# Delta keys kept unnormalised, with one transposition instead of two, and gate tiles copied out of their bank by ScalarE

## The chip, the cores and the metric

The kernel runs on one core of a Trainium2 chip. The metric is the device time of one execution in microseconds, taken as the median of several runs. A core has TensorE (PE, with its weight loads as PEld), VectorE (DVE), ScalarE (ACT), GpSimd (POOL) and SyncE (SP), which issues the DMAs. Each works through its own queue of instructions in order.

## The reference

One hybrid decoder layer for 512 tokens of width 2048, in float32. A modulated RMS norm gives h; one wide product of h feeds a sliding-window attention branch, a gated delta-rule branch and two merge gates; the branches are projected, merged and added to x. What matters here is the delta-rule branch, with 16 key heads and 32 value heads of 128:

```python
d_qkv = causal_conv_silu(d_qkv, conv_w)
dq, dk, dv = jnp.split(d_qkv, [DN_KEY, 2 * DN_KEY], axis=-1)
dq = jnp.repeat(l2_norm(dq...), rep, axis=2)
dk = jnp.repeat(l2_norm(dk...), rep, axis=2)     # x * rsqrt(sum(x * x) + EPS), by token and head
beta = jax.nn.sigmoid(db)
...
L = jnp.where(strict, einsum(k_beta, k) * decay, 0.0)     # in chunks of 64 tokens
t_inv = triangular_solve(eye + L, eye)
u = t_inv @ v_beta
w = t_inv @ (k_beta * jnp.exp(g)[..., None])
...
v_new = u_c - w_c @ S                                      # scan over the chunks
o = qd_c @ S + qk_c @ v_new
S = S * gl_c + kd_c.T @ v_new
...
o = rms_norm(o, dn_norm_w) * jax.nn.silu(dz)
```

Every key is divided by its own norm over the 128 channels, which depends on the token alone.

## The kernel before, in words

The work goes in stages: a start-up (norm, modulation, the first four key tiles), the keys stage (`delta_keys`), the attention stage, the heads stage (`delta_heads`) and a tail with the large output products. In the first stages the unit is a channel tile: 128 output channels by all 512 tokens, 16 steps of the contraction with three products each (L280 to L282: high by high, high by low, low by high part), so 48 matmuls of 128x512 into one PSUM bank. Two banks take turns, so the third tile may start only when the first one's bank has been read. A weight tile of 1 MB is loaded by SP (L213, two or three buffers), and split in halves by ScalarE (whi, L68) and VectorE (wlo, L69), three halves deep.

After every second contraction step `pump` runs (L98): it lets the background work take one step. Everything beside the products is a generator that says with `yield n` after how many pumps its next step is due; the solve, the sums of weight quadrants (q, L1505 to L1516) and the modulation gate (gate_bc, L1863) run at a pace of their own. Each engine's queue is then ordered when the kernel is built; in the keys stage TensorE's instructions may be reordered against the program too.

The keys stage takes 12 key tiles (four more come from start-up) and 18 output-gate tiles (z). First come four gates, then the keys 4 to 7 back to back, then keys and gates in turn, then the gates that are left.

A key tile (`keys`, L752) goes through these steps. The convolution (`conv`, L655): ScalarE scales by one tap (L659), VectorE adds three shifted taps out of the bank (L662), then tanh (L667) and a product (L669) give y, channels by tokens. Four transpositions give ptk, tokens by channels, in PSUM; ScalarE sums its squares (L801). VectorE takes the inverse root in eleven small operations (L763 to L81, rk). ScalarE writes k, the tokens scaled by rk (L768, four activations). Four more transpositions give ptkT, and ScalarE copies it to kT (L776), the normalised key, channels by tokens. The product pkk of kT with itself (L783) is multiplied by VectorE into the decay tiles E of two heads (L786), and the results go to scratch memory (L793, L794). k and kT go there too, for the heads stage. The decay tiles are loaded by SP as broadcasts of g_rows (L806), masked by GpSimd (L811), and run through exponentials by ScalarE (L817). ptk, ptkT and pkk share a PSUM pool of two buffers.

A gate tile (`z_gate`, L316): ScalarE takes the tanh of half the bank (L320), VectorE multiplies (tanh + 1) by the bank (L322), and the result is stored (L324). The same function serves the gates of the later stages, with another pool tag.

The solve (L819) inverts the triangular matrices of 16 heads at a time on VectorE: it loads beta by rows (bet, L831) and the tiles lt_d, multiplies the columns by minus beta (nb), and at the end the inverse by beta. The heads stage loads k, kT and the inverses, turns each value tile into token order (vt, L900, one copy by ScalarE), and scans four blocks of 128 tokens.

Of the kernel before, what the change touches and what calls it, by code (L numbers as in the profile page):

```python
# [7 lines left out]
F32 = mybir.dt.float32  # L8
F32R = mybir.dt.float32r
I32 = mybir.dt.int32  # L10
AF = mybir.ActivationFunctionType
ALU = mybir.AluOpType
# [4 lines left out]
P = 128  # L17
T = 512
D = 2048
KT = D // P  # L20
NTB = T // P
EPS = 1e-6
KH = 16
VH = 32
QH = 32
HD = 64
# [26 lines left out]
class Layer:  # L53
# [262 lines left out]
    def z_gate(self, h, ps):  # L316
        nc = self.nc
        pool, tag, bufs = self.zpool
        th = pool.tile([P, T], F32, tag=tag, name="zth", bufs=bufs)
        nc.scalar.activation(th, ps, AF.Tanh, scale=0.5)  # L320
        yield 1
        nc.vector.scalar_tensor_tensor(out=th, in0=th, scalar=1.0, in1=ps, op0=ALU.add, op1=ALU.mult)  # L322
        yield 3
        self.behind(nc.sync.dma_start(out=self.z_d[h], in_=th))  # L324

# [253 lines left out]
    def gates(self, sp):  # L579

        nc, a, dnc = self.nc, self.a, self.dnc
# [14 lines left out]
            nc.tensor.transpose(pb[:, c, :], ba[:, c * P : (c + 1) * P], self.ident)  # L596
        nc.vector.tensor_copy(out=bd, in_=pb[:, :, 0 : 2 * VH])
        nc.vector.tensor_tensor(out=bd, in0=pb[:, :, 2 * VH :], in1=bd, op=ALU.add)
        beta = self.beta = dnc.tile(S, F32, name="beta")
        e = sp.tile(S, F32, name="ge")  # L600
        nc.scalar.activation(e, bd[:, :, 0:VH], AF.Exp, scale=-1.0)
        nc.vector.tensor_scalar(out=e, in0=e, scalar1=1.0, scalar2=None, op0=ALU.add)
# [69 lines left out]
    def delta_keys(self):  # L672
        tc = self.tc
        dram = self.dram
        self.lt_d = dram.tile([2, 2, 16, 4, HD, HD], F32, name="lt_d")
        self.lab_d = dram.tile([VH, HD, 4, HD], F32, name="lab_d")
        self.ta_d = dram.tile([2, 16, 4, HD, HD], F32, name="ta_d")
        self.ts_d = dram.tile([2, 2, 16, 4, HD, HD], F32, name="ts_d")
        self.kT_d = dram.tile([KH, P, T], F32, name="kT_d")
        self.k_d = dram.tile([KH, P, T], F32, name="k_d")  # L680
        self.o_d = dram.tile([VH, P, T], F32, name="o_d")
        with ExitStack() as sa:
            self.ptp = sa.enter_context(tc.tile_pool(name="ptp", bufs=2, space=PSUM, reuse_waits="tile"))
            self.zpool = (sa.enter_context(tc.tile_pool(name="gwk", bufs=1, reuse_waits="tile")), "zth", 1)
            wk = sa.enter_context(tc.tile_pool(name="dnA", bufs=2, reuse_waits="tile"))
            gp = sa.enter_context(tc.tile_pool(name="gates", bufs=1, reuse_waits="tile"))
            gates = self.gates(gp)
            self.go(gates, next(gates))
            gt = sa.enter_context(tc.tile_pool(name="gatew", bufs=1, reuse_waits="tile"))
            self.beside(self.gate(gt), 0.26, "gate")  # L690
            kr = sa.enter_context(tc.tile_pool(name="kraw", bufs=1, reuse_waits="tile"))
            self.third_raw(kr, self.last_key)
            self.due += [self.split_half] * 2
            self.keys_done = []
            for g in range(NST):
                self.go(self.keys(wk, g, self.acc_k[g]), 10 + 8 * g)
            for h in ZAHEAD[:NFIRST]:
                self.z_tile(h)
            self.solved = []
            self.solves = self.paced(self.solve_all(), 0.41)  # L700
            ws = sa.enter_context(tc.tile_pool(name="wsumk", bufs=1, reuse_waits="tile"))
            sums = self.paced(self.weight_sums(ws, [0], 12.5), 1.0)
            rwk = sa.enter_context(tc.tile_pool(name="rwk", bufs=1, reuse_waits="tile"))
            self.go(self.rope_tables(rwk, rwk), 40)
            for kind, j in self.mixed():
                if kind == "k":
                    self.go(self.keys(wk, j, self.channel_tile(f"k{j}")), 0)
                else:
                    self.z_tile(j)
            self.drain("gate")  # L710
            self.drain_slow(sums)
            self.drain_live()
# [39 lines left out]
    def keys(self, wk, g, ps):  # L752

        nc = self.nc
        y = wk.tile([P, T], F32, tag="y", name="y", bufs=3)
        yield from self.conv(wk, ps, 16 + g, y)
        yield 2
        pt = self.ptp.tile([P, T], F32, tag="tp", name="ptk")
        self.transpose4(pt, lambda c: y[:, c * P : (c + 1) * P])
        ss = self.sumsq(wk, pt)  # L760
        yield 3
        E = [self.decay_load(wk, 2 * g + e) for e in range(2)]
        nc.vector.tensor_scalar(out=ss, in0=ss, scalar1=EPS, scalar2=None, op0=ALU.add)  # L763
        rk = self.rsqrt(wk, ss, NTB, "rk")
        yield 4
        k = wk.tile([P, NTB, P], F32, tag="k", name="k")
        for c in range(NTB):
            nc.scalar.activation(k[:, c, :], pt[:, c * P : (c + 1) * P], AF.Copy, scale=rk[:, c : c + 1])  # L768
        for e in range(2):
            self.decay_mask(E[e])  # L770
        yield 4
        pt = self.ptp.tile([P, T], F32, tag="tp", name="ptkT")
        self.transpose4(pt, lambda c: k[:, c, :])
        nc.sync.dma_start(out=self.k_d[g], in_=k.rearrange("p c d -> p (c d)"))
        kT = wk.tile([P, T], F32, tag="kT", name="kT")
        nc.scalar.copy(out=kT, in_=pt)  # L776
        for e in range(2):
            self.decay_exp(E[e], 2 * g + e)
        yield 2
        pk = self.ptp.tile([P, NTB, P], F32, tag="tp", name="pkk")  # L780
        for c in range(NTB):
            sl = slice(c * P, (c + 1) * P)
            self.pe(nc.tensor.matmul(pk[:, c, :], lhsT=kT[:, sl], rhs=kT[:, sl], start=True, stop=True))  # L783
        nc.sync.dma_start(out=self.kT_d[g], in_=kT)
        for e in range(2):
            nc.vector.tensor_tensor(out=E[e], in0=pk, in1=E[e], op=ALU.mult)  # L786
        yield 2
# [31 lines left out]
    def solve(self, wk, b, eng):  # L819
# [3 lines left out]
            yield 1.0  # L823
        A = wk.tile([P, HD, HD], F32, tag="A", name="A", bufs=1)
        bet = wk.tile([P, HD], F32, tag="bet", name="bet", bufs=1)
        for k2 in range(2):
            s = slice(k2 * HD, (k2 + 1) * HD)
            nc.sync.dma_start(
                out=A[s].rearrange("u j i -> u (j i)"), in_=self.lt_d[b, k2].rearrange("h c j i -> (h c) (j i)")
            )  # L830
            nc.sync.dma_start(  # L831
                out=bet[s],
                in_=self.b_rows.rearrange("h (c k i) -> k (h c) i", c=4, k=2)[k2, b * HD : (b + 1) * HD, :],
            )
        yield 8.0
        nb = wk.tile([P, HD], F32, tag="nbet", name="nbet", bufs=1)
        self.behind(eng.tensor_scalar(out=nb, in0=bet, scalar1=-1.0, scalar2=None, op0=ALU.mult))
        for j in range(0, HD, 16):
            s = slice(j, j + 16)
# [52 lines left out]
    def values(self, wk, g, e, ps, st):  # L892
        nc = self.nc
        y = wk.tile([P, T], F32, tag="y", name="yv", bufs=3)
        yield from self.conv(wk, ps, 32 + 2 * g + e, y)
        yield 3
        pt = self.ptp.tile([P, T], F32, tag="tp", name="ptv")
        self.transpose4(pt, lambda c: y[:, c * P : (c + 1) * P])
        vt = wk.tile([P, NTB, P], F32, tag="vt", name="vt", bufs=4)
        nc.scalar.copy(out=vt.rearrange("p c d -> p (c d)"), in_=pt)  # L900
        st[f"v{e}"] = vt

    def queries(self, wk, g, ps, st):
# [1056 lines left out]
```

## Time and profile before

| | us |
|---|---|
| median of three runs (lowest, highest) | 2884.59 (2880.28, 2886.27) |
| the profiled execution | 2872.44 |
| its span from first to last instruction | 2870.7 |

The profiled execution has a granted TensorE clock of 0.988 in the mean. The page gives the busy time of each engine with its share of the span; the tables by stretch give the busy time of each engine within a window, the number of instructions in brackets, then the granted TensorE clock, the share in which the 16 DMA engines are busy, and GB/s. A line of the waits reads: the engine and line that waited, what released it, the sum in us, the number of waits, the longest. A line of the timeline is start and duration in us, engine, line, operation, output and inputs, and in square brackets the idle time before it. A line of a group gives the count, the busy sum, the mean in ns of one, and the idle time before them. Matmuls overlap each other, so the distance of their starts is what one costs, not the duration.

### The profile page before, as it was taken

The numbers are of one execution on the slowest core, as the hardware profiler recorded it, in microseconds if no ns is written. First come the engines' busy times: TensorE is split into PE (matmuls) and PEld (weight loads), VectorE is DVE, ScalarE is ACT, GpSimd is POOL, SyncE is SP. The second block draws the span as 40 slices with busy tenths as digits, with TensorE's granted clock in tenths as the row PEclk, the third lists the DMA queues.
The fourth block names the chain that finished last, engine by engine and source line by source line (L and its number), as shares of the span: only waits on it lengthen the run. The fifth ranks groups of instructions, "written<-read, shape, count | busy, mean of one in ns | idle before, by whom it ended". The sixth has DMA issues, their size and how long they took to land.

```text
span 2870.7 us, 39644 instructions
## 1 busy us (share of the span) xinstructions
PE 2769.7 (96%) x13864; PEld 2237.7 (78%) x13864; DVE 2212.2 (77%) x3594; ACT 1318.3 (46%) x2649; POOL 139.6 (5%) x124
## 2 busy tenths in 40 slices
PE   8999898999999999999989999998999999999999
PEld 6788676777777777778878888777878878788887
DVE  7887787788778778899777777758666878887876
ACT  5565342234544434434534444445444645454543
POOL 0010000011000001101000001000000000000000
PEclk9999999999999999999999999999999999999999
DMA  9889888554565458999999999966798999998875
GB/s 401 346 272 286 294 301 275 163 188 136 182 174 186 160 169 294 289 317 305 313 300 309 301 309 293 297 193 205 251 312 311 325 324 327 352 347 279 293 250 189
DMA packets 332652, 776.39 MB, mean 270 GB/s; under 512 B 88066, under 2 KB 112258, under 8 KB 287394
## 3 DMA queue, kind: packets, MB, share of 16 engines
q1 hardware_dynamic: 332452, 773.86, 79.9%
q8 instruction: 109, 1.79, 0.2%
q14 instruction: 91, 0.75, 0.1%
HBM read 588.84 MB, written 182.66 MB: 269 GB/s over the span
## 4 chain that ended last, share of the span: by engine, by line
PE 44%; DMA 7%; DVE 3%; issue 1%; SPq 1%; ACT 1%; POOL 0%; DVEq 0%; POOLq 0%; ACTq 0%
PE m L281 9%; PE m L282 9%; PE m L280 9%; PE mm L280 4%; PE mm L282 4%; PE mm L281 4%; DMA s_d<-q 3%; DMA q<-in_w_q 1%; DVE wlo L69 1%; PE pv L1004 1%; PE pp L994 1%; PE pod L1021 1%; DMA b_d<-o 0%; PE pod L1017 0%; PE pod L1020 0%
## 5 line engine op out<-in xcount | busy, mean ns | idle before, releaser
L69 DVE TENSOR_TENSOR wlo<-raw,whi 128x1024 fp32r<-128x1024 f32 x588 | 721.2, 1228 | 347.6 <-ACT whi L68 334.8
L68 ACT CAST whi<-raw 128x1024 fp32r<-128x1024 f32 x588 | 617.0, 1051 | 758.3 <-PE m L282 352.4
L280 PE MATMUL mm<-hh,whi 128*128 128x512 f32 x2016 | 832.0, 413 | 12.9 <-DVE zth L322 12.9
L282 PE MATMUL mm<-hh,wlo 128*128 128x512 f32 x2016 | 795.1, 394 | 0.0
L281 PE MATMUL mm<-hl,whi 128*128 128x512 f32 x2016 | 792.9, 393 | 0.0
L280 PEld LDWEIGHTS mm<-hh,whi 128*128 128x128 f32 x2016 | 383.2, 190 | 102.0 <-DVE zth L322 15.6
L282 PEld LDWEIGHTS mm<-hh,wlo 128*128 128x128 f32 x2016 | 382.3, 190 | 84.5 <-issue 0.2
L281 PEld LDWEIGHTS mm<-hl,whi 128*128 128x128 f32 x2016 | 383.8, 190 | 70.8 <-issue 0.5
L1511 DVE TENSOR_TENSOR q<-q,q 128x512 f32<-128x512 f32 x384 | 270.5, 704 | 48.0 <-DMA q<-in_w_q 34.5
L849 DVE TENSOR_TENSOR atmp<-A 128x62 f32<-128x62 f32 (+30 forms) x124 | 109.6, 884 | 0.5
L857 DVE TENSOR_TENSOR A<-A,atmp 128x62 f32<-128x62 f32 (+30 forms) x124 | 107.8, 869 | 0.5
L811 POOL TENSOR_SCALAR_AFFINE_SELECT E<-E 128x512 f32<-128x512 f32 x64 | 55.9, 884 | 1020.1 <-DMA E<-g_rows 927.6
L817 ACT ACTIVATE E<-E,neg_g 128x128 f32<-128x128 f32 x256 | 82.2, 400 | 16.3 <-POOL E L811 13.2
L280 PE MATMUL m<-whi,hh 128*128 128x512 f32 x192 | 77.3, 404 | 8.1 <-ACT whi L68 6.7
L281 PE MATMUL m<-wlo,hh 128*128 128x512 f32 x192 | 76.6, 399 | 1.3 <-DVE wlo L69 1.3
L1022 ACT COPY osb<-pod 128x256 f32<-128x256 f32 x64 | 23.7, 371 | 117.2 <-PE pod L1021 93.1
L1009 ACT ACTIVATE vs<-pv,kd 128x128 f32<-128x128 f32 x96 | 30.1, 365 | 102.5 <-PE pv L1004 102.1
L282 PE MATMUL m<-whi,hl 128*128 128x512 f32 x192 | 75.9, 396 | 0.0
L662 DVE SCALAR_TENSOR_TENSOR yv<-mm,convh,yv 128x511 f32<-128x511 f32 (+2 forms) x96 | 71.3, 743 | 1.0
L281 PE MATMUL m<-wlo,f2h 128*128 128x512 f32 x160 | 62.5, 391 | 0.9 <-DVE wlo L69 0.9
L1807 ACT ACTIVATE sm<-sm,mx,rs 128x128 f32<-128x128 f32 x128 | 61.5, 482 | 2.9 <-DVE mx L1802 2.4
L280 PE MATMUL m<-whi,f1h 128*128 128x512 f32 x160 | 62.7, 392 | 0.0
(436 smaller groups left out, 4781.8 us busy)
## 6 DMA issues: line engine op xcount, KB each, us to landing
raw<-in_w_ch SPq DMA_DIRECT2D x126, 1024.0 KB
q<-in_w_q SPq DMA_DIRECT2D x384, 256.0 KB
s_d<-q SPq DMA_DIRECT2D x384, 256.0 KB
raw<-s_d SPq DMA_DIRECT2D x96, 1024.0 KB
raw<-in_w_q SPq DMA_DIRECT2D x72, 1024.0 KB
wa<-in_w_ada_ss SPq DMA_DIRECT2D x32, 1024.0 KB
gw<-in_w_ada_gate SPq DMA_DIRECT2D x16, 1024.0 KB
E<-g_rows SPq DMA_DIRECT2D x64, 256.0 KB
```

Of the source, the lines that this page charges most:

```text
L68: h = self.nc.scalar.copy(out=hi, in_=src)
L69: l = self.nc.vector.tensor_tensor(out=lo, in0=src, in1=hi.bitcast(F32), op=ALU.subtract)
L280: self.pe(nc.tensor.matmul(ps, lhsT=wh, rhs=xh, start=first, stop=False))
L281: self.pe(nc.tensor.matmul(ps, lhsT=wh, rhs=xl, start=False, stop=False))
L282: self.last_mm = self.pe(nc.tensor.matmul(ps, lhsT=wl, rhs=xh, start=False, stop=last))
L662: nc.vector.scalar_tensor_tensor(out=y[:, s:], in0=ps[:, : T - s], scalar=w[:, j : j + 1], in1=y[:, s:], op0=ALU.mult, op1=ALU.add)
L811: self.last_mask = self.nc.gpsimd.affine_select(out=E, in_=E, pattern=[[0, NTB], [1, P]], compare_op=ALU.is_ge, fill=NEG, base=0, channel_ ...
L817: self.nc.scalar.activation(E[:, c, :], E[:, c, :], AF.Exp, bias=self.neg_g[:, c, h : h + 1])
L849: eng.tensor_tensor(out=t, in0=A[:, m : m + 1, m + 1 :].to_broadcast([P, m, n]), in1=A[:, :m, m : m + 1].to_broadcast([P, m, n]), op=ALU.mult,
L857: self.behind(eng.tensor_tensor(out=A[:, :m, m + 1 :], in0=A[:, :m, m + 1 :], in1=t, op=ALU.add))
L1511: self.behind(self.nc.vector.tensor_tensor(out=q[f], in0=q[x], in1=q[y], op=ALU.add))
L1807: nc.scalar.activation(t, t, AF.Exp, scale=r[:, h : h + 1], bias=mx[:, h : h + 1], accum_out=den[:, h : h + 1])
```

## The change

The key is no longer divided by its norm n. Scratch memory and the heads stage get the raw key, and what this changes is put right in other places: beta is divided by n squared (sum of squares plus EPS) wherever it is used in the inverse, and the values are multiplied by n. The scan's new values then come out divided by n, which the raw key makes good where it meets them (in the state's update and in the product with the queries).

In `keys`: the raw y goes to kT_d right after its transposition; ScalarE writes one plain copy k of ptk right after the sums of squares; VectorE computes n (knorm), 1/n squared (inv) and scales the two heads' columns of neg_beta in place; SP stores inv twice, once per head, as 512 single words each; the second transposition and kT go; pkk is the product of y with itself; and the yields become 2, 3, 2, 2, 2, 2 where they were 2, 3, 4, 4, 2, 2. y gets a fourth buffer. In the solve two more loads bring inv, and one more product makes bet. In the heads stage vt is written by four scaled activations, one per block of 128 tokens. In `z_gate`, in the keys stage alone, ScalarE copies the bank to zc right after the tanh, and VectorE's product reads zc.

```diff
@@ z_gate
         nc.scalar.activation(th, ps, AF.Tanh, scale=0.5)
+        if tag == "zth":
+            z = pool.tile([P, T], F32, tag="zc", name="zc", bufs=bufs)
+            nc.scalar.copy(out=z, in_=ps)
+        else:
+            z = ps
         yield 1
-        nc.vector.scalar_tensor_tensor(out=th, in0=th, scalar=1.0, in1=ps, op0=ALU.add, op1=ALU.mult)
+        nc.vector.scalar_tensor_tensor(out=th, in0=th, scalar=1.0, in1=z, op0=ALU.add, op1=ALU.mult)
@@ keys
-        y = wk.tile([P, T], F32, tag="y", name="y", bufs=3)
+        y = wk.tile([P, T], F32, tag="y", name="y", bufs=4)
...
         self.transpose4(pt, lambda c: y[:, c * P : (c + 1) * P])
+        nc.sync.dma_start(out=self.kT_d[g], in_=y)
         ss = self.sumsq(wk, pt)
+        k = wk.tile([P, NTB, P], F32, tag="k", name="k")
+        nc.scalar.copy(out=k.rearrange("p c d -> p (c d)"), in_=pt)
         yield 3
...
         rk = self.rsqrt(wk, ss, NTB, "rk")
-        yield 4
-        k = wk.tile([P, NTB, P], F32, tag="k", name="k")
-        for c in range(NTB):
-            nc.scalar.activation(k[:, c, :], pt[:, c * P : (c + 1) * P], AF.Copy, scale=rk[:, c : c + 1])
+        nc.vector.tensor_tensor(out=self.knorm[:, :, g], in0=ss, in1=rk, op=ALU.mult)
+        inv = wk.tile([P, NTB], F32, tag="inv", name="inv")
+        nc.vector.reciprocal(out=inv, in_=ss)
+        both = inv.unsqueeze(2).to_broadcast([P, NTB, 2])
+        nb = self.neg_beta[:, :, 2 * g : 2 * g + 2]
+        nc.vector.tensor_tensor(out=nb, in0=nb, in1=both, op=ALU.mult)
+        nc.sync.dma_start(out=self.k_d[g], in_=k.rearrange("p c d -> p (c d)"))
+        for e in range(2):
+            nc.sync.dma_start(out=self.inv_d[2 * g + e].rearrange("(c p) -> p c", p=P), in_=inv)
+        yield 2
         for e in range(2):
             self.decay_mask(E[e])
-        yield 4
-        pt = self.ptp.tile([P, T], F32, tag="tp", name="ptkT")
-        self.transpose4(pt, lambda c: k[:, c, :])
-        nc.sync.dma_start(out=self.k_d[g], in_=k.rearrange("p c d -> p (c d)"))
-        kT = wk.tile([P, T], F32, tag="kT", name="kT")
-        nc.scalar.copy(out=kT, in_=pt)
+        yield 2
         for e in range(2):
             self.decay_exp(E[e], 2 * g + e)
...
-            self.pe(nc.tensor.matmul(pk[:, c, :], lhsT=kT[:, sl], rhs=kT[:, sl], start=True, stop=True))
-        nc.sync.dma_start(out=self.kT_d[g], in_=kT)
+            self.pe(nc.tensor.matmul(pk[:, c, :], lhsT=y[:, sl], rhs=y[:, sl], start=True, stop=True))
@@ solve
+            for dst, rows in ((bet, self.b_rows), (nb, self.inv_d)):
...
+        self.behind(eng.tensor_tensor(out=bet, in0=bet, in1=nb, op=ALU.mult))
         self.behind(eng.tensor_scalar(out=nb, in0=bet, scalar1=-1.0, scalar2=None, op0=ALU.mult))
@@ values
-        nc.scalar.copy(out=vt.rearrange("p c d -> p (c d)"), in_=pt)
+        for c in range(NTB):
+            nc.scalar.activation(vt[:, c, :], pt[:, c * P : (c + 1) * P], AF.Copy, scale=self.knorm[:, c, g : g + 1])
```

More of the change, by code (lines that the diff above doesn't have):

```diff
@@ L598, in gates @@
         nc.vector.tensor_tensor(out=bd, in0=pb[:, :, 2 * VH :], in1=bd, op=ALU.add)
-        beta = self.beta = dnc.tile(S, F32, name="beta")
+        beta = sp.tile(S, F32, name="beta")
         e = sp.tile(S, F32, name="ge")
@@ L680, in delta_keys @@
         self.k_d = dram.tile([KH, P, T], F32, name="k_d")
+        self.inv_d = dram.tile([VH, T], F32, name="inv_d")
+        self.knorm = self.dnc.tile([P, NTB, KH], F32, name="knorm")
         self.o_d = dram.tile([VH, P, T], F32, name="o_d")
@@ L825, in solve @@
         bet = wk.tile([P, HD], F32, tag="bet", name="bet", bufs=1)
+        nb = wk.tile([P, HD], F32, tag="nbet", name="nbet", bufs=1)
         for k2 in range(2):
@@ L830, in solve @@
             )
[L831 to L834, printed above, removed]
+            for dst, rows in ((bet, self.b_rows), (nb, self.inv_d)):
+                nc.sync.dma_start(
+                    out=dst[s], in_=rows.rearrange("h (c k i) -> k (h c) i", c=4, k=2)[k2, b * HD : (b + 1) * HD, :]
+                )
         yield 8.0
-        nb = wk.tile([P, HD], F32, tag="nbet", name="nbet", bufs=1)
+        self.behind(eng.tensor_tensor(out=bet, in0=bet, in1=nb, op=ALU.mult))
         self.behind(eng.tensor_scalar(out=nb, in0=bet, scalar1=-1.0, scalar2=None, op0=ALU.mult))
```

## The prediction

> **What bounds the kernel now.** I read the page first, then the busy time by stretches, then TensorE's waits in the stretch that the change touches.
>
> ```profile
> span 2870.7 us, 39644 instructions
> PE 2769.7 (96%) x13864; PEld 2237.7 (78%) x13864; DVE 2212.2 (77%) x3594; ACT 1318.3 (46%) x2649; POOL 139.6 (5%) x124
> ```
>
> TensorE is busy for 96% of the span, so a gain can only be work taken off TensorE or idle time given back to it. The stretches are the keys stage while keys come back to back (120 to 280 us), the keys stage with keys and output gates in turn (280 to 540, with 400 to 440 out of its middle), and the heads stage (1085 to 1960).
>
> ```profile
> core 0: us, PE busy (x) PEld busy (x) DVE busy (x) ACT busy (x) POOL busy (x), PEclk, DMA share, GB/s
> 120.00:280.00 160.00, 158.02 (x776) 130.23 (x775) 126.76 (x261) 96.05 (x255) 14.49 (x18) 1.00 0.87 284
> 280.00:540.00 260.00, 230.97 (x1017) 186.99 (x1016) 198.44 (x288) 90.21 (x209) 14.54 (x16) 0.95 0.83 273
> 400.00:440.00 40.00, 36.01 (x171) 29.61 (x170) 37.47 (x53) 16.15 (x37) 1.25 (x2) 1.00 0.91 304
> 1085.00:1960.00 875.00, 846.88 (x4611) 698.95 (x4609) 667.25 (x1172) 385.68 (x1024) 79.19 (x64) 0.99 0.89 290
> ```
>
> In the first stretch TensorE is full (158 of 160 us): there the bound is its own work. In the second it is idle for 29 of 260 us and its clock is granted at 0.95 in the mean. VectorE fills 76% of that stretch, the DMA engines 83%, ScalarE 35%. The waits of TensorE from 120 to 540 us say where the idle time goes (in all, number of waits, longest).
>
> ```profile
> PE mm L280 <- DVE zth L322: 12.9, 4, 5.8
> PE ptk L329 <- DVE E L786: 8.7, 1, 8.7
> PE pkk L783 <- ACT kT L776: 4.7, 5, 1.7
> PE ptkT L329 <- ACT k L768: 2.1, 2, 1.8
> PE pkk L783 <- DVE E L786: 1.6, 1, 1.6
> ```
>
> These 30 us are the whole idle time of the stage. Each of the five has a place in the diff: the accumulation bank of a gate tile is freed by VectorE (L322); the second transposition waits for ScalarE's scaled copy k, and the product pkk for the copy kT; and three users (ptk, ptkT, pkk) share two PSUM buffers, so that ptk waits for VectorE to read an older pkk (L786).
>
> **The change part by part.** *The second transposition.* One set of four costs TensorE this:
>
> ```profile
> 204.05 0.40 PE L282 MATMUL mm<-hh,wlo 128*128 128x512 f32 x1
> 204.29 0.60 PE L329 MATMUL ptkT<-ident,k 128*128 128x128 f32 x4
> 204.64 0.48 PE L280 MATMUL mm<-hh,whi 128*128 128x512 f32 x1
> 204.96 0.40 PE L281 MATMUL mm<-hl,whi 128*128 128x512 f32 x1
> 205.19 0.40 PE L282 MATMUL mm<-hh,wlo 128*128 128x512 f32 x1
> ```
>
> From 204.05 to 204.96 is 0.91 us, in which two products start; the next two starts lie 0.23 apart where nothing comes between (205.19 after 204.96), so the set costs 0.91 - 0.46 = 0.45 us. Sixteen keys: **-7.2 us**, all of it on the path where TensorE is full.
>
> *The waits behind it.* pkk reads y, ready since before the first transposition, and waits for neither k nor kT: 4.7 + 2.1 = **-6.8 us**. ptk and pkk are the only users of the two PSUM buffers but for the gate sums, so a ptk no longer needs an older pkk to be read: 8.7 + 1.6 = **-10.3 us**.
>
> *The gate tile's copy.* ScalarE copies the tile out right behind the tanh, and the bank is free then, not after VectorE's product. The longest of the four waits:
>
> ```profile
> 474.62 0.58 ACT L320 ACTIVATE zth<-mm 128x512 f32<-128x512 f32 x1
> ```
>
> ```profile
> 478.53 0.68 DVE L322 SCALAR_TENSOR_TENSOR zth<-zth,mm 128x512 f32<-128x512 f32 x1
> ```
>
> The bank came free at 479.2. A copy as long as the tanh ends at about 475.8, which saves 3.4 of 5.8 us, 0.6 of the wait. I take 0.6 of all four: **-7.7 us**. The ends are 0 (the tanh is itself what is late) and 12.9.
>
> *The clock after the waits.* Four short stretches run at half clock, each at or behind one of these waits.
>
> ```profile
> 315.00:328.60 13.60, 4.94 (x17) 3.97 (x16) 10.79 (x19) 6.96 (x21) 0.00 (x0) 0.50 0.54 193
> 376.40:383.20 6.80, 5.10 (x12) 4.05 (x13) 6.04 (x9) 1.56 (x2) 0.00 (x0) 0.50 0.87 266
> 478.90:482.20 3.30, 2.94 (x7) 2.37 (x8) 1.97 (x3) 0.00 (x0) 0.00 (x0) 0.50 0.60 170
> 506.30:509.60 3.30, 3.30 (x9) 2.58 (x8) 0.81 (x2) 0.57 (x1) 0.00 (x0) 0.51 0.95 252
> ```
>
> ```profile
> 378.69 0.63 PE L281 MATMUL mm<-hl,whi 128*128 128x512 f32 x1
> 379.12 0.63 PE L282 MATMUL mm<-hh,wlo 128*128 128x512 f32 x1
> ```
>
> There a product starts every 0.43 us and not every 0.23. Of the 45 matmuls in these rows some 36 are such products (17 + 12 + 7 + 9, less the short ones in the first): 36 x 0.2 = 7 us. With most of the waits gone I take 5 of it: **-5 us**. The Trainium skill ("TensorE: Matmul & The Clock Gate", Part 1) puts the drop after an idle window of about 3.4 us; by it two of the four drops would not belong to these waits and the refund would be about half. The row at 376.4 follows a shorter wait and does not bear that out.
>
> Together -7.2 - 6.8 - 10.3 - 7.7 - 5 = **-37 us**.
>
> *What comes on top.* ScalarE: per key the four scaled copies and kT go, one plain copy comes; per gate tile one copy comes; in the heads stage each of 32 value tiles takes four scaled copies for one plain copy.
>
> ```profile
> 207.36 1.14 ACT L768 ACTIVATE k<-ptk,rky 128x128 f32<-128x128 f32 x4
> ```
>
> ```profile
> L320 ACT ACTIVATE zth<-mm 128x512 f32<-128x512 f32 x18 | 10.6, 591 | 5.0 <-DMA z_d<-zth 5.0
> L776 ACT COPY kT<-ptkT 128x512 f32<-128x512 f32 x16 | 9.3, 583 | 11.7 <-PE ptkT L329 11.7
> ```
>
> ```profile
> L900 ACT COPY vt<-ptv 128x512 f32<-128x512 f32 x32 | 18.7, 585 | 0.0
> ```
>
> Keys: 16 x (1.14 + 0.58 - 0.58) = -18 us, gates 18 x 0.59 = +11 us: ScalarE gains a little. Heads: 32 x (1.14 - 0.59) = +18 us on an engine that is 44% busy there, beside a TensorE that is idle for 28 of 875 us. Hidden by that slack it costs 0, wholly exposed 18; the matmul that reads vt comes at least two steps later, so I take **+3**.
>
> VectorE: three small operations more per key (knorm, the reciprocal, the scaled beta).
>
> ```profile
> L80 DVE TENSOR_TENSOR rkt<-rkt,ss 128x4 f32<-128x4 f32 x48 | 8.1, 168 | 1.0
> ```
>
> ```profile
> L1812 DVE RECIPROCAL den<-den x16: 193/203/204, 624.6 to 1049.0; 128x8 f32<-128x8 f32 x16
> ```
>
> 0.17 + 0.20 + 0.17 = 0.54 us, 16 times 9 us, nothing of it in front of TensorE directly. The solve adds two loads of 16 KB and one small product a batch: nothing.
>
> *The decay chain comes earlier against its load.* Between loading E and its exponentials lay 4 + 4 steps of the pump and now 2 + 2; a step is six products, 1.37 us, so 5.5 us in place of 11; VectorE's use of E comes 6 steps (8.2 us) behind the load in place of 10.
>
> ```profile
> L817 ACT ACTIVATE E<-E,neg_g x8: 399/402/416, 451.5 to 453.5; 128x128 f32<-128x128 f32 x8
> L806 SPq DMA_DIRECT2D E<-g_rows x2: 429/431/433, 438.1 to 438.6; - x2
> L811 POOL TENSOR_SCALAR_AFFINE_SELECT E<-E x2: 637/637/637, 444.4 to 445.0; 128x512 f32<-128x512 f32 x2
> L786 DVE TENSOR_TENSOR E<-pkk,E x2: 681/682/684, 455.8 to 456.4; 128x512 f32<-128x512 f32 x2
> ```
>
> The masks ended 7.5 us after the first issue and the eight exponentials take about 2.4. So ScalarE can stand up to 2 us and VectorE up to 1.7 us per key at these, with casts of weights (whi, wlo) and tanh queued behind. Weights are cast three halves ahead, which covers it while VectorE has time to spare.
>
> *What it does to VectorE.* If the second stretch lost 33 of the 37 us, VectorE would be busy 198 + 6 of 227 us, 90%, before any standing. At 78% to 79% (first stretch) TensorE lost 1%, at 94% (400 to 440 us) 10%. At 90% I read some 6% of 227, with the standing at E on top: **+14 us** of new waits. Ends: 0 and the 30 us of waits that went.
>
> *The stores of inv.* 32 DMAs write 512 single words each, and wait on SP's queue for the reciprocal, with weight and gate loads behind them. The trace has no single-word store; nearest are pieces of 256 bytes, in this 2 us stretch nearly alone:
>
> ```profile
> DMA packets 1387, 0.57 MB, mean 285 GB/s; under 512 B 1358, under 2 KB 1358, under 8 KB 1358
> q1 hardware_dynamic: 1386, 0.55, 102.4%
> ```
>
> 2 us x 16 engines / 1387 = 23 ns a piece; 16384 pieces are 23.6 us of all 16 engines, spread over the stage. The DMA work of the two stretches is 160 x 0.87 + 260 x 0.83 = 355 us; 379 in 398 us is 95%, still below full. Issuing costs SP
>
> ```profile
> L793 SPq DMA_DIRECT2D lt_d<-E x64: 574/609/2596, 170.9 to 482.7; - x64
> L774 SPq DMA_DIRECT2D k_d<-k x16: 319/374/602, 163.8 to 471.9; - x16
> ```
>
> about 0.24 us per 128 pieces, so some 1.1 us each, 35 us of SP's time in 400. I take 0 for the path, ends 0 and the rival below.
>
> Sum: -37 + 3 + 14 = **-20 us**. The profiled execution took 2872.44 us (span 2870.7), 12 below the median of the runs, 2884.59; against that median the forecast is **2865 us**.
>
> **The rivals.** *VectorE takes over wholly* (0.17): the 30 us of waits come back behind other names and only transpositions and a little clock are won, -7.2 - 3 + 3, so about -7 us, 2878. For it: 94% busy from 400 to 440, and exponentials nearer to their load. Against: the 8.7 us wait stood in a stretch in which VectorE was not full (10.79 of 13.6).
>
> *The tanh is what is late* (0.12): then the gate copy frees nothing, 7.7 and half of the clock's 5 stay, and the gain is 10 us, 2875. For it: tanh and copy share ScalarE's queue with exponentials and casts.
>
> *Single-word stores are dear* (0.13, the slower side): the place is the DMA engines between 120 and 540 us.
>
> ```profile
> 240.00:280.00 40.00, 40.00 (x199) 33.29 (x198) 29.13 (x54) 20.01 (x54) 4.02 (x6) 1.00 0.96 314
> ```
>
> The fullest stretch of the stage has a DMA share of 0.96, with TensorE full beside it. The stage's 355 us plus the stores must fit in 420 us at that share; that leaves 48 us, 47 ns a word. Beyond it weights come late and the stage grows. At three times the 256-byte price, 70 ns, it takes (355 + 72) / 0.96 = 445 us: +25, with the heads' 3 about 2912. Against: a small piece costs 23 ns even in a crowd, and single words have less to carry. The Trainium skill ("DMA: Bandwidth & Descriptors", Specifications) says that below 512 bytes the engine reads, modifies and writes; the 256-byte stores would be under that rule already, at 23 ns, and no run here shows a single word.
>
> *The order on the queues shifts elsewhere* (0.06): the heads stage loses 10 us or more of its 28 idle ones again, no gain or +5, 2887.
>
> **How the numbers follow.** Forecast 0.52 at 2865, the tanh case 0.12 at 2875, VectorE 0.17 at 2878 (half of it inside 0.2%), stores 0.13, order 0.06 (half slower). 0.2% is 5.8 us, about what a measurement of this kernel tells from no change. Faster by more: 0.52 + 0.12 + 0.08 = 0.72; same 0.09 + 0.03 = 0.12; slower 0.13 + 0.03 = 0.16. The low end takes the 37 us whole, 2847; the high end reaches over the VectorE and order cases, 2888, and leaves most of the dear stores out.
>
> **What would show it.** Right: no ptkT or kT; in TensorE's waits from 120 to 540 us no line with kT, k or zth and no 8 us wait of ptk; the attention stage begins some 20 us earlier; fewer half-clock stretches; heads as long as before. VectorE's share of the late stretch near 90%. Wrong: new waits of TensorE for wlo or whi of the same sum (VectorE), a DMA share near 0.97 with weights landing late (stores), or zth's wait replaced by one for zc.

## The result, and the profile after

The changed kernel takes 2986.4 us (median of 4 runs, 2978.57 to 2990.09) where the kernel before takes 2882.6 beside it (4 runs): a ratio of 1.0355, with a 95% interval of 1.0331 to 1.038. It is 3.5% slower, and outside the range of 2847 to 2888. The profiled execution took 2987.6 us. Its page begins so:

```profile
span 2985.8 us, 39579 instructions
...
PE 2788.8 (93%) x13800; PEld 2250.1 (75%) x13800; DVE 2214.6 (74%) x3644; ACT 1329.3 (45%) x2697; POOL 141.2 (5%) x124
...
DMA packets 349869, 776.53 MB, mean 260 GB/s; under 512 B 105282, under 2 KB 129474, under 8 KB 304610
...
PE 55%; DMA 26%; DVE 10%; SPq 3%; issue 3%; ACT 2%; POOL 0%; DVEq 0%; ACTq 0%; POOLq 0%
```

TensorE's share fell from 96% to 93% with 64 matmuls fewer. There are 17,200 more packets under 512 bytes (88,066 before), and on the chain that ended last a quarter of the span is transfers.

Where the time lies is read from the row of ksq, ScalarE's first work of the attention stage, in the kernel before, and then in the changed one (number, shortest/median/longest ns, first and last start).

```profile
L1683 ACT ACTIVATE ksq<-mm x2: 592/594/597, 541.3 to 553.5; 128x512 f32<-128x512 f32 x2
```

```profile
L1695 ACT ACTIVATE ksq<-mm x2: 585/590/596, 634.4 to 646.6; 128x512 f32<-128x512 f32 x2
```

Attention begins 93 us later, of 115 us between the two spans. So the keys stage has most of it. Its stretches in the changed kernel, with the columns that the prediction explained:

```profile
120.00:280.00 160.00, 137.21 (x621) 111.96 (x620) 108.81 (x250) 75.49 (x191) 8.84 (x12) 0.93 0.89 205
280.00:540.00 260.00, 188.71 (x802) 154.07 (x800) 170.84 (x288) 81.66 (x191) 18.85 (x18) 0.85 0.98 236
```

This is the reading on which everything turns. The DMA engines are busier than before (0.89 and 0.98, before 0.87 and 0.83), yet they move less (205 and 236 GB/s, before 284 and 273). Busy time of a DMA engine is the time that its packets took, not what they carried: here packets stand. TensorE, VectorE and ScalarE all do less in the same time. TensorE's waits from 120 to 540 us:

```profile
PE mm L280 <- ACT zc L323: 42.7, 7, 11.6
PE ptk L334 <- DVE y L674: 24.0, 5, 8.9
PE ptk L334 <- DVE E L796: 16.0, 2, 15.7
PE pkk L794 <- ACT k L770: 8.0, 3, 4.1
```

The names that the prediction looked for (kT, ptkT, zth) are gone. In their place stand the copy zc, y and E, and they are three times as long. Behind zc stands ScalarE's own queue:

```profile
ACT E L827 <- POOL E L821: 47.5, 15, 10.9
ACT zth L320 <- DMA z_d<-zth: 42.5, 8, 12.6
```

The exponentials wait for GpSimd's masks, and eight times a mask waited for a load of E; the tanh waits for a store that has not landed (5.0 us before). It is transfers that are late. The stores of inv, and what the DMA engines do around the first pair of them:

```profile
L783 SPq DMA_DIRECT2D inv_d<-inv x32: 370/432/1087, 156.3 to 554.2; - x32
```

```profile
157.00:159.00 2.00, 2.00 (x11) 1.59 (x10) 2.00 (x5) 0.93 (x4) 1.78 (x2) 1.00 1.45 134
159.00:167.00 8.00, 8.00 (x43) 6.82 (x42) 6.60 (x17) 2.84 (x9) 0.68 (x1) 1.00 0.92 34
170.00:174.00 4.00, 3.81 (x22) 2.98 (x21) 3.58 (x9) 2.15 (x9) 1.26 (x2) 1.00 1.01 408
```

The view of the transfers, first from 157 to 158 us, then for the last two of these stretches:

```profile
DMA packets 954, 0.04 MB, mean 37 GB/s; under 512 B 938, under 2 KB 938, under 8 KB 954
q1 hardware_dynamic: 954, 0.04, 52.9%
...
DMA packets 50, 0.27 MB, mean 34 GB/s; under 512 B 7, under 2 KB 7, under 8 KB 20
...
DMA packets 551, 1.63 MB, mean 408 GB/s; under 512 B 64, under 2 KB 64, under 8 KB 448
```

The two stores were issued at 156.25 and 156.68 us. These views count a packet, with all its time, where it begins. Most of the words begin from 157 to 158, and they are quick: 1 us x 16 engines x 0.529 / 954 = 8.9 ns a packet. It is the packets behind them that stand. In the 8 us from 159 only 50 begin, 34 GB/s, and their time fills the engines to 0.92; from 170 on it is 408 GB/s again. In the first of these stretches a packet took 8 us x 16 engines x 0.92 / 50 = 2.4 us, in the second 4 x 16 x 1.01 / 551 = 0.12. Their sizes explain less than a factor of two of that (5.4 and 3.0 KB in the mean). TensorE still runs on (8.00 of 8.00 us) from weights loaded ahead; the next pair is issued at 177, and so on for 16 keys. Later nothing is ahead any more: from 376 to 384 us TensorE is busy for 1.1 of 8 us, at 99 GB/s.

### The profile page after: what moved, and what is told of

The parts are those of the page before. It is cut to its first block, busy times and chain, and to the rows that moved or that the text cites. A ratio compares the mean times of both kernels' runs of the same rounds, so it can differ in the third digit from the quotient of the medians.

```text
span 2985.8 us, 39579 instructions
## 1 busy us (share of the span) xinstructions
PE 2788.8 (93%) x13800; PEld 2250.1 (75%) x13800; DVE 2214.6 (74%) x3644; ACT 1329.3 (45%) x2697; POOL 141.2 (5%) x124
## 4 chain that ended last, share of the span: by engine, by line
PE 55%; DMA 26%; DVE 10%; SPq 3%; issue 3%; ACT 2%; POOL 0%; DVEq 0%; ACTq 0%; POOLq 0%
PE m L281 8%; PE m L282 8%; PE mm L280 8%; PE m L280 8%; PE mm L281 8%; PE mm L282 8%; DMA q<-in_w_q 7%; DMA s_d<-q 6%; DVE wlo L69 2%; DMA kT_d<-y 2%; DMA inv_d<-inv 1%; DMA E<-g_rows 1%; DMA gw<-in_w_ada_gate 1%; SPq L1517 1%; DMA z_d<-zth 1%
## 5 line engine op out<-in xcount | busy, mean ns | idle before, releaser
L1021 ACT ACTIVATE vs<-pv,kd 128x128 f32<-128x128 f32 x96 | 30.1, 365 | 96.6 <-PE pv L1016 96.2
```

## The experiments

The theory after the result (A): the stores of single words stop all other traffic, and that is the whole loss. The rival (B): VectorE or ScalarE is overloaded by the new order, and late transfers follow from it. Every time is set against the kernel before on the same chip: 2878.2 to 2879.2 us in the groups of runs below, 2882.6 beside the changed kernel. So the changed kernel is 104 us over the kernel before, and where a version below is compared with it, each is first set against its own kernel before. Most ratios have an interval of some 0.0012 on either side, 3.5 us, so two such versions can be told apart from about 5 us; without stores the interval is similar, with whole rows it is 0.002, and a single execution has none.

**Without the stores.** The solve reads constant rows (c_rows) in place of inv.

```diff
-        for e in range(2):
-            nc.sync.dma_start(out=self.inv_d[2 * g + e].rearrange("(c p) -> p c", p=P), in_=inv)
 ...
-            for dst, rows in ((bet, self.b_rows), (nb, self.inv_d)):
+            for dst, rows in ((bet, self.b_rows), (nb, self.c_rows)):
```

> The changed kernel without the 32 stores of inv; the solve multiplies by constant rows (0.001, stored once as whole rows) in place of inv, so the outputs are not the layer's. Theory A (the single-word stores stop all other transfers, about 10 us for each pair of stores in the trace of after, 16 pairs): the keys stage falls from 512 us to 400 or less, the time from 2987 to 2865 to 2890. Theory B (the shorter chain: exponentials now wait for the masks, 73 us of ScalarE, and hold up what is queued behind them): the stores are a bystander, the time stays above 2950.

2888.8 us, 1.0036 [1.0023, 1.0049]: 10 us over the kernel before where the change is 104 over it, so 94 us are gone with 32 DMAs. B falls as the main cause. But A falls as the whole of it: the change stays slower without the stores, and attention begins at 538.5 us where it began at 541.3 before, so the keys stage did not come down to 400 us.

**Whole rows.** The inverses of eight keys are gathered, transposed by TensorE and stored as pieces of 2 KB.

```diff
-        inv = wk.tile([P, NTB], F32, tag="inv", name="inv")
+        inv = self.inv_t[:, :, g]
 ...
-        for e in range(2):
-            nc.sync.dma_start(out=self.inv_d[2 * g + e].rearrange("(c p) -> p c", p=P), in_=inv)
 ...
+        if g % 8 == 7:
+            pr = self.ptp.tile([P, T], F32, tag="tp", name="pinv")
+            for c in range(NTB):
+                self.pe(nc.tensor.transpose(pr[0:8, c * P : (c + 1) * P], self.inv_t[:, c, g - 7 : g + 1], self.ident))
+            rows = wk.tile([P, T], F32, tag="th", name="irows")[0:8]
+            nc.vector.tensor_copy(out=rows, in_=pr[0:8])
+            for e in range(2):
+                nc.sync.dma_start(out=self.inv_d.rearrange("(g e) t -> e g t", e=2)[e, g - 7 : g + 1], in_=rows)
```

> The changed kernel with inv gathered on chip for eight keys, turned by TensorE into rows and stored as 16 pieces of 2 KB per batch instead of 8192 single words; all else as changed. Theory A: as e1 within 8 us, so 2865 to 2895, and the first fair test of what was forecast for the rest (keys stage 20 us shorter than before's 419). Theory B: above 2950. The heads stage (881 us in after, 869 before) should stay near 881 if the scaled copies of the values are its loss, near 869 if it only suffered from something else.

2892.2 us, 1.0053 [1.0032, 1.0073]. The same numbers get to memory at 3 us over no stores, which is within the noise. So it is the form, not the data.

**The words alone, on the kernel before.**

```diff
+        for e in range(2):
+            nc.sync.dma_start(out=self.inv_d[2 * g + e].rearrange("(c p) -> p c", p=P), in_=rk)
```

> The kernel before with 32 stores of single words added (rk, to a scratch that nobody reads); the result is the layer's. Theory A: the keys stage grows by 90 us or more, since nothing else of the change is there to be blamed: 2970 to 3000. Theory B: within 15 us of before, 2885 to 2900.

2965.1 us, 1.0304 [1.0284, 1.0324]: 86 us with nothing else changed, 5 us short of the range expected. That is the loss shown from the other side.

**Words 64 bytes apart** (the solve reads constants here and in the next three).

```diff
-        self.inv_d = dram.tile([VH, T], F32, name="inv_d")
+        self.inv_d = dram.tile([VH, T, 16], F32, name="inv_d")
 ...
-            nc.sync.dma_start(out=self.inv_d[2 * g + e].rearrange("(c p) -> p c", p=P), in_=inv)
+            nc.sync.dma_start(out=self.inv_d[2 * g + e, :, 0].rearrange("(c p) -> p c", p=P), in_=inv)
```

> As e1 (constant rows in the solve, so outputs are not the layer's) but with the 32 stores of inv in, each word 64 bytes from the next, so that no two words of a store lie in one line of 64 bytes. If words are dear because neighbours fall into one line and have to be done one after the other: the time falls to 2865 to 2900, as e1. If every single word is dear wherever it lies: it stays at 2970 to 3000.

2905.0 us, 1.0096 [1.0075, 1.0118]: 16 us over no stores, 5 above the first of the two ranges, with as many pieces as the change and the same reads on the chip. So neither the number of pieces nor the reading is the price; words side by side in memory are. (The words of a store now also spread over 32 KB in place of 2; the two are not told apart.)

**One store for each key instead of two.**

```diff
-        for e in range(2):
-            nc.sync.dma_start(out=self.inv_d[2 * g + e].rearrange("(c p) -> p c", p=P), in_=inv)
+        nc.sync.dma_start(out=self.inv_d[2 * g].rearrange("(c p) -> p c", p=P), in_=inv)
```

> The changed kernel with half the stores of inv (one of the two heads of each key; the solve reads constants). If each word stops the other traffic for about 10 ns, one after another, half the words cost half of the 98 us between the changed kernel and the one without stores: 2889 + 49, about 2938 us. If the first store after a pause is dear and the second rides along, about 2980 us; if only two stores close together collide, about 2895 us.

2972.0 us (one execution), 93 over the kernel before: half the words cost 83 of the 94 us. The proportional reading missed by 34 us. The one in which the second store rides along came within 8: it costs some 11 us more.

**Pieces of 16 bytes**, 128 to a store.

```diff
-            nc.sync.dma_start(out=self.inv_d[2 * g + e].rearrange("(c p) -> p c", p=P), in_=inv)
+            nc.sync.dma_start(out=self.inv_d[2 * g + e].rearrange("(p c) -> p c", c=NTB), in_=inv)
```

> The changed kernel with the same 32 stores of inv of 2 KB each, but as 128 pieces of 16 bytes (four words of a partition side by side) where it has 512 of 4 bytes; the order of the words in memory differs and the solve reads constants. If each piece costs the same, one after another, a quarter of the 98 us: 2889 + 24, about 2913 us. If what costs is two engines writing into one line of memory, pieces of 16 bytes still share lines by four: between 2895 and 2930. If it is the number of stores, 2986.

2907.7 us (one execution), 19 us over no stores. It lies within 5 us of the first forecast and inside the range of the second, so by itself it does not decide between them.

**Words 16 bytes apart**, four to a line of 64 bytes.

```diff
-        self.inv_d = dram.tile([VH, T], F32, name="inv_d")
+        self.inv_d = dram.tile([VH, T, 4], F32, name="inv_d")
 ...
-            nc.sync.dma_start(out=self.inv_d[2 * g + e].rearrange("(c p) -> p c", p=P), in_=inv)
+            nc.sync.dma_start(out=self.inv_d[2 * g + e, :, 0].rearrange("(c p) -> p c", p=P), in_=inv)
```

> The changed kernel with the same 32 stores of 512 single words, each word 16 bytes from the next (the solve reads constants): four words to a line of 64 bytes, where the change has 16 (97 us over no stores) and the run with 64 bytes between has one (16 us). If the cost goes with the words that share a line: 16 + 81 x 3/15, about 32 us over no stores, 2921. If any two neighbours in a line cost the whole: 2986. If lines do not matter and only whole pages of memory do: between 2930 and 2960.

2918.9 us (one execution), 30 us over no stores where the reading by lines said 32. One word to 64 bytes costs 16, four cost 30, sixteen cost 94: the price goes with how close together the words are written. That 64 bytes are the stretch that counts is not shown: any larger one would give these three runs the same proportions. The half fits too, if the two stores of a pair, which go to different rows, can wait side by side; no record shows that waiting.

**The rest of the change.** From here on the version with whole rows (2892.2) is the base. First without the gate copy:

```diff
-        if tag == "zth":
-            z = pool.tile([P, T], F32, tag="zc", name="zc", bufs=bufs)
-            nc.scalar.copy(out=z, in_=ps)
-        else:
-            z = ps
+        z = ps
```

> The version with stores of whole rows (2892 us in the first runs), without ScalarE's copy of the gate tiles. The forecast's reading (the bank came free at VectorE's product, the copy frees it 3.4 us earlier and saves 0.6 of each wait): 2892 + 7.7, about 2900 us, and TensorE's waits at L280 are put down to VectorE's zth again. The rival (tanh and copy are themselves late, queued behind exponentials which wait for the masks of E): the same 2892 us within 4, or a little less since 18 copies of 0.59 us go from ScalarE.

2900.1 us, 1.0072 [1.0055, 1.0089]: by these medians the copy saves 7.9 us, where the forecast said 7.7. The two intervals overlap, so the agreement is worth little. The waits show it more plainly: without it TensorE waits 29.1 us for VectorE's zth, with it 11.3 for zc.

**Four steps around the masks again.**

```diff
-        yield 2
+        yield 4
         for e in range(2):
             self.decay_mask(E[e])
-        yield 2
+        yield 4
```

> The version with stores of whole rows, with 4 steps of the pump on either side of the masks as before the change, in place of 2. If ScalarE and VectorE stand at E because its load and mask have not ended (5.5 us allowed where some 7.5 are needed), the keys stage falls from 419 us toward 410 and the whole to some 2884 us. If VectorE's load is what delays TensorE (the rival from the forecast), nothing changes: 2892 us within 4. If the longer life of a pt buffer matters, neither: pt is read before these steps.

2870.6 us, 0.9975 [0.9961, 0.9989]. The two steps that were saved on either side of the masks cost 21.6 us, and this version beats both kernels (the kernel before by 8 us). TensorE's waits from 120 to 540 us, with two steps and then with four:

```profile
PE mm L280 <- ACT zc L323: 11.3, 6, 3.9
PE ptk L334 <- DVE y L674: 8.3, 1, 8.3
PE ptk L334 <- DVE E L795: 6.2, 1, 6.2
PE pgate L1890 <- DVE gate_bc L1882: 3.9, 1, 3.9
```

```profile
PE ptk L334 <- DVE E L795: 18.9, 1, 18.9
PE mm L280 <- ACT zc L323: 12.2, 7, 3.9
```

Attention begins at 541.8 us with two steps and 533.2 with four, so 9 of the 14 us between the two profiled executions lie in the keys stage; these waits explain only part of them (ScalarE's waits for the masks, too, only fall from 10.8 to 8.0 us), and why attention is 5 us longer with two steps stays open.

**Plain value copies** (the factor n is left out of the values).

```diff
-        for c in range(NTB):
-            nc.scalar.activation(vt[:, c, :], pt[:, c * P : (c + 1) * P], AF.Copy, scale=self.knorm[:, c, g : g + 1])
+        nc.scalar.copy(out=vt.rearrange("p c d -> p (c d)"), in_=pt)
```

> The version with stores of whole rows, with the value tiles copied once and plain, as before the change; the factor n is left out of the values, so the outputs are scaled wrongly. If the 128 scaled copies of ScalarE are what makes the heads stage 7 to 10 us longer, it goes back to some 871 us and the whole to 2884 us. If the order of the work on the queues, or the values' other users, makes it longer, the time stays at 2892 us within 3.

2893.1 us, 1.0044 [1.003, 1.0058], no different from 2892.2: the 96 additional operations cost nothing that can be seen, which leaves room for the 3 us forecast but not for 18.

**Where the other gains stayed.** In the version with four steps one wait of 18.9 us holds TensorE. Around it, on GpSimd and then VectorE:

```profile
310.56 2.81 POOL L828 TENSOR_SCALAR_AFFINE_SELECT E<-E 128x512 f32<-128x512 f32 x2 [37.75 <-DMA E<-g_rows]
```

```profile
321.31 2.34 DVE L1882 SCALAR_TENSOR_TENSOR gate_bc<-gw,silu_c,gate_bc 128x2048 f32<-128x2048 f32 x1
323.57 1.28 DVE L795 TENSOR_TENSOR E<-pkk,E 128x512 f32<-128x512 f32 x2
```

TensorE stands from 306.1 to 325.0. The load of E landed late (the mask at 310.6), and the exponentials ended at 314.7. The product of pkk and E then stood for 9 us more behind the solve, casts and gate_bc on VectorE, until 323.6, and ptk, two tiles on in the same two buffers, had to wait for it. So pkk was given a bank of its own, in this version, in the same without the gate copy, and in the kernel before:

```diff
-        pk = self.ptp.tile([P, NTB, P], F32, tag="tp", name="pkk")
+        pk = self.psc.tile([P, NTB, P], F32, tag="sc", name="pkk")
```

> The version with stores of whole rows and 4 steps on either side of the masks (2871 us), with the product pkk in one of four PSUM banks that stand empty in the keys stage, instead of one of the two buffers that ptk uses. If the gain of the transposition went into the wait of ptk for VectorE's reading of pkk (18.9 us in one wait), that wait goes, the keys stage falls from 410 us to some 392 to 396 and the whole to 2852 to 2856. If VectorE or the late load of E is the bound whatever the bank, the wait comes back elsewhere: 2867 to 2873.

2869.9 us, 0.9974 [0.9964, 0.9985]: no gain over 2870.6. The long wait went, and in its trace two others have taken the 18.9 us over:

```profile
PE mm L280 <- ACT zc L323: 18.6, 8, 4.4
PE ptk L334 <- DVE y L674: 9.4, 1, 9.4
```

> The same without ScalarE's copy of the gate tiles. If the copy is worth what it was worth with 2 steps (7.9 us), some 8 us above the version with it: about 2862. If the copy only helps while the other wait moves the tanh, equal within 3. Set against the kernel before with the same bank for pkk it gives the value of the missing transposition and its two waits alone: by the forecast's terms (7.2 + 6.8) 14 us less; by the rival (VectorE fills up, the waits come back) 0 to 3 less.

2885.9 us, 1.0023 [1.0011, 1.0035]. Without the copy it is 16 us slower, twice what was expected: here TensorE waits 30.1 us for zth in place of 18.6 for zc.

> The kernel before with pkk alone in a bank of its own. The 8.7 + 1.6 us of waits of ptk and pkk for VectorE's E go: 2879 - 10, about 2869 to 2872, if the slot is what delays; nothing if VectorE or the load of E does (then the same work is waited for by another name).

2883.1 us, 1.0018 [1.0007, 1.003]: no faster than before, rather 4 us slower. The buffer delays nothing by itself. Between the last two lies the second transposition with its copies, and with them the change's small operations, scaled value copies and rows of inv. The pair differs by 3 us in the wrong direction, within the noise; 14 us less it is not.

**TensorE's work or VectorE's?** One version has the second set of transpositions put back (into the bank of pkk, which overwrites it), the other an additional VectorE operation for each E.

```diff
+        self.transpose4(pk.rearrange("p c d -> p (c d)"), lambda c: y[:, c * P : (c + 1) * P])
```

> The version with whole rows and 4 steps around the masks (2871 us) with a second set of four transpositions per key put back, of y into the bank of pkk, which overwrites it: TensorE's work of the old second transposition, without its waits and copies. If TensorE's work is on the path all through the keys stage, as the forecast's term of 7.2 us has it: 2878. If work taken off TensorE only turns into waiting there: 2871 within 3.

```diff
+            nc.vector.tensor_tensor(out=E[e], in0=E[e], in1=E[e], op=ALU.max)
```

> The same version with one more VectorE operation behind each product of pkk with E (the maximum of E with itself, which leaves it as it is): 32 operations of about 0.7 us, 22 us more of VectorE in the keys stage. If VectorE takes over (the forecast's first rival), most of the 22 us show: 2885 to 2893. If VectorE has room and the waits come from the order in its queue or from late loads: 2871 to 2877.

2876.6 us, 0.9998 [0.9985, 1.0011], and 2871.8 us, 0.9974 [0.9961, 0.9988], beside 2870.6. What each put in, from its own trace:

```profile
L334 PE MATMUL pkk<-ident,y 128*128 128x128 f32 x64 | 9.6, 272 | 0.0
```

```profile
L796 DVE TENSOR_TENSOR E<-E 128x512 f32<-128x512 f32 x32 | 21.5, 686 | 0.3
```

64 transpositions cost 6 us, with an uncertainty of about 5, near the forecast's 7.2. 21.5 us of VectorE cost 1 us, within the noise: in the version with four steps VectorE has room, and there the first rival falls. What its queue does in a bad order is another matter, as the 9 us above show.

**A third bank for the sums**, in the version with pkk apart, without the gate copy and then with it.

```diff
-        return pool.tile([P, T], F32, tag="mm", name=name)
+        return pool.tile([P, T], F32, tag="sc" if pool is self.psc else "mm", name=name)
 ...
+                self.banks.append(self.psc)
                 self.delta_keys()
+                self.banks.pop()
```

> The version with whole rows, 4 steps and pkk in a bank of its own (2870 us with the copy of the gate tiles, 2886 without), without the copy, but with the sums of the keys stage going round three PSUM banks in place of two. If TensorE waits for a bank that is freed late, the waits for zth or zc (12 to 30 us in the stage) go: 2855 to 2865. If VectorE's and ScalarE's queues are what is late, the waits only come later: 2870 to 2886.

2876.6 us, 0.9991 [0.998, 1.0003]: 9 us better than with two banks. TensorE's waits from 280 to 540 us, then ScalarE's:

```profile
PE mm L282 <- DVE wlo L69: 10.6, 5, 4.8
PE mm L280 <- ACT whi L68: 8.0, 5, 2.6
PE mm L280 <- DVE zth L323: 5.6, 3, 2.4
```

```profile
ACT whi L68 <- DMA raw<-in_w_ch: 37.5, 10, 11.4
```

zth is nearly gone, and TensorE now waits for weights (wlo, whi), which wait for their load. That wait of ScalarE's is not in its list for the version with four steps, which goes down to 1.2 us. By these waits the weight loads are the next limit; no run tries them.

> Whole rows, 4 steps, pkk in a bank of its own (2870 us), with the gate copy and with three banks for the sums too. If a bank freed late is what is left of the waits in the keys stage (some 12 us for zc): 2858 to 2864. If copy and third bank are two ways to the same gain: 2870 within 3.

2877.9 us, 1.0002 [0.9991, 1.0013], which neither forecast had. The copy adds nothing to a third bank, and a third bank makes the version with the copy 8 us slower (2869.9 with two). TensorE's waits here are again those for weights (wlo 11.3 us, whi 10.5); why the third bank brings them is open.

**E loaded five steps earlier**, in the version with four steps.

```diff
         yield from self.conv(wk, ps, 16 + g, y)
+        E = [self.decay_load(wk, 2 * g + e) for e in range(2)]
         yield 2
 ...
         yield 3
-        E = [self.decay_load(wk, 2 * g + e) for e in range(2)]
```

> Whole rows, 4 steps around the masks (2871 us), with the load of E issued 5 steps earlier, ahead of the first transposition. If the masks still wait for late loads in the stretch from 300 to 330 us (8 us there, behind which TensorE stands for 18.9): 2856 to 2864. If 4 steps were enough but for that one place, or the earlier loads only push the weights back: 2871 within 3.

2869.2 us, 0.9966 [0.9953, 0.9979]. It is the fastest version of all, 0.3% below the kernel before, but not to be told from 2870.6. The long wait halved: the masks now run at 304.5 us, but the exponentials still end at 313.2 and the product starts at 316.1, behind other work on ScalarE and VectorE. Waits for y of nearly the same sum as what was left came in:

```profile
PE ptk L334 <- DVE E L795: 10.1, 1, 10.1
PE ptk L334 <- DVE y L674: 9.6, 3, 4.2
```

## Why the prediction was wrong

Two steps put the forecast on the wrong side, and a third kept the mended change from what was hoped. The parts, each against the kernel before beside it: the change +104; whole rows +13, so the single words cost 90; whole rows with four steps -8, so the shortened steps cost 22; the rest is -8. 90 + 22 - 8 = 104.

- **The step that failed: the stores of inv, "I take 0 for the path".** It took the words' own time on the DMA engines, at the price of a 256-byte piece, 23 ns, spread over 16 engines, and asked whether the engines have that time to spare. Their own time was less than that, 8.9 ns each. What the sum put at nothing is the time that every packet behind them stands: 2.4 us in place of 0.12 in the 8 us after the first pair, and 94 us of the kernel for 16384 words, about 6 ns a word with nearly nothing else moving. As a price per word over 16 engines that is some 92 ns, four times the price taken. "Single words have less to carry" was true of their own time and said nothing of the packets behind. The dear-stores rival (0.13) had the place and the sign, and its sign came, a DMA share of 0.98; but at 70 ns it came to +25 only, since it too let words fill engines as other packets do. They do not: one word to 64 bytes costs 16 us, sixteen cost 94. The sum by the DMA share (0.83 + stores, still below 1) could not see it, because that share counts standing packets as busy. Issuing, put at 1.1 us a store, took 0.43 us (median of the 32).
- **The shortened steps, inside the "+14 us of new waits".** The place was right in so far as the steps alone cost 22 us. The reason given for most of the 14, VectorE at 90%, was not: VectorE fills 77% of the second stretch with two steps and 79% with four, and there 21.5 us more of VectorE cost 1 us. The prediction saw at most 2 us of standing for each key and mostly hid it. How the 22 us come about is shown only in part, as said at that run.
- **The gate copy, -7.7:** 7.9 by the medians with two steps (the intervals overlap), 16 with four steps and pkk apart, nothing with a third bank. So the agreement of 7.9 with 7.7 is partly luck. The rival that only the tanh is late falls, though ScalarE's queue is what TensorE waits for now (zc, 12.2 us in the version with four steps).
- **The second transposition, -7.2:** right in size where it was tried by itself (6 us for putting it back). The pair that differs by it and by the rest of the change without the copy (2885.9 against 2883.1) does not show it; that difference stays open.
- **The waits behind it (-6.8), the PSUM buffers (-10.3) and the clock (-5):** the names went, the time did not. "A ptk no longer needs an older pkk to be read" was wrong as stated: with two tiles a key in two buffers, ptk still gets the buffer of an earlier pkk, and that wait grew from 8.7 to 18.9 us. Nor was the buffer the cause: with a bank of its own the wait moved to y. The clock in the second stretch was 0.95 before and 0.91 to 0.95 in the versions with whole rows (0.94 with four steps). TensorE's listed waits add up to 31 us before and to 33 with four steps.
- **Heads, +3:** nothing that can be measured.
- **VectorE as the bound (0.17)** falls by the run with more VectorE work, for the version with four steps; with two it was not tried. "The 30 us of waits come back behind other names" is nevertheless what happened, through the order on ScalarE's and VectorE's queues and, with a third bank, through the weight loads.

## What to carry to other kernels

Price a store by its form and not by its bytes: words that lie side by side in memory, written one by one from many partitions, nearly stopped the other transfers, while TensorE's transposing them and a few stores of whole rows did the same for about 3 us. And do not price it by its own packets alone; ask what it does to those behind it. Read DMA share and GB/s together: a share that rises while the rate falls means that packets stand. And when a wait goes from a stage with several queues just in time, ask what stands right behind it before you count it as won: here, with pkk apart, the copy alone gained 16 us and a third bank alone 9, and both together 8.

## What the runs showed of the hardware

Neighbouring single-word stores were the surprise. The words themselves took about 9 ns each on a DMA engine (954 packets, nearly all of them words, 8.9 ns in the mean), and for 8 us behind the first 1024 of them 34 GB/s moved where it was 408 a few us later. The cost grew with how close together the words lay (16, 30 and 94 us for 1, 4 and 16 words to 64 bytes). The Trainium skill ("DMA: Bandwidth & Descriptors", Specifications) says that transfers below 512 bytes are done by read, modify and write. The runs agree in so far as words close together cost more, as they would if each had to read what its neighbour wrote; but pieces of 16 bytes and words 64 bytes apart are under the same rule and cost 19 and 16 us, so the rule alone does not tell them apart, and no run here shows the reading itself.
